# The passes over a long input placed one by one behind the weight splits of a short projection, and a convolution placed behind operand splits

## The chip, the cores and the metric

The kernel runs on one core of a Trainium2 chip. The metric is the device time of one execution in microseconds (us). The engines in the text are PE (TensorE, matmuls), DVE (VectorE), ACT (ScalarE), POOL (GpSimd) and SP (SyncE, which issues the DMA transfers).

## The reference, cut to what matters

One layer of a hybrid encoder is applied to two inputs that share all weights: a long one of 1024 tokens and a short one of 512, each with 16 learned tokens ahead. Everything is float32.

```python
n = rms_norm(h, g_mix)
qa, ka, va, qb, kb, vb = split(n @ w_in)              # one projection, 18 blocks of 128 columns
oa = softmax_attention(rope(rms_norm(qa)), rope(rms_norm(ka)), va)      # grouped queries, 2-D rotary
ob = rms_norm((softmax(qb0 @ kb0) - lam * softmax(qb1 @ kb1)) @ vb)     # differential attention
h = h + concat(oa, ob) @ w_out
n = rms_norm(h, g_ffn)
gate = conv3(n @ w_ff_gate) + conv_b                  # depthwise over positions, width 3
h = h + (gelu(gate) * (n @ w_ff_up)) @ w_ff_down
y = rms_norm(h, g_final)[16:]
```

## The kernel before

**Arithmetic.** A float32 operand is held as a rounded part "hi" and a rest "lo". `split` (L103) makes hi with a copy on ACT (L106) and lo = x - hi with a subtraction on DVE, or on POOL where the caller asks for it (L107). `mm3` (L110) makes a product of three matmuls, hi*hi, hi*lo and lo*hi (L113 to L115). `dense` runs it over the 8 blocks of the contraction, so one product of a weight with a chunk of tokens is 24 matmuls.

**Stages.** First the projection of the short input (s = 1) by itself. Then `merge` alternates the generators of two stages by their estimated work: attention of the short input with the projection of the long one (s = 0, named p0), then attention of the long input with the output product and feed-forward of the short. The long input's output product, its feed-forward (`conv_glu_long`, eleven groups of two feature blocks, with products by the schemes of Winograd and Strassen) and the down product come after.

**Projection.** Eight tiles x of the input are loaded (L217). For each, a *pass* makes xhi on ACT (L223) and xlo on DVE (L224), and squares x on ACT (L227). The short input's squares go into a PSUM bank by matmuls; the long one's are added to a tile acc on POOL (L232), and three matmuls with ones (L241, chunks of 384, 384 and 272 tokens) turn acc into the mean. `rsqrt_newton` (L89) makes the reciprocal root: Ln, Exp and Square on ACT (L95 to L97), two steps on DVE (L98, L99). The 18 weights go one after another, KA, VA, QA, VB and so on in pairs, then KB and QB four times. `load_weight` loads one into w_f (L167), of which there is one buffer here, and splits it into w_hi and w_lo (two buffers each). The queries and keys get their norm and rotary (t at L295, then L258 to L261), the values are transposed on PE by L322 from t (L316).

**Attention.** ps_s = k*q (L406, L407), a running maximum with the copy out of PSUM (p, L408), the exponent (L413), transposes of p (L431), their split (L106, L107) and the product with v (L441 to L446).

**Order.** The program is written stage by stage, and a scheduler with a simulated timeline sets one fixed sequence for each engine; an engine then runs its sequence in order and waits at each instruction for what it needs. `tc.issue_after(ins)` adds an edge to this scheduling: what is written inside it stands behind `ins` where both are on one engine. It adds no wait. PSUM banks in the early stages are mm = 2, s = 3, t = 2, o = 1; the short projection uses s and t, the long one mm alone.

Before, the only such edge for the long passes is this one, the short norm's last steps:

```python
for ins in g.norm_of_short:
    order.enter_context(tc.issue_after(ins))
```

## Time and profile before

| what | value |
|---|---|
| median of 3 runs | 2137.26 us (2137.07 to 2148.71) |
| the profiled execution | 2142.05 us, its span 2140.2 us |
| busy: PE | 2046.2 us, 96% of the span |
| busy: DVE | 1738.0 us, 81% |
| busy: ACT | 1158.9 us, 54% |
| busy: POOL | 556.1 us, 26% |

The busy time of an engine is the sum of what ran on it; what it lacks to the span is waiting. All times of the rows below count from the start of the span. In a row such as "t<-ps_s,rstd", the output stands left of the arrow and the inputs right, by the program's names; L295 is a line of the kernel, often of a helper that many places call. "SPq" is the queue in which SP issues transfers.

### The profile page before, as it was taken

What the parts mean: (1) busy time and instruction counts of PE and PEld (TensorE: products, weight loads), DVE (VectorE), ACT (ScalarE), POOL (GpSimd) and SP (SyncE); (2) the same over time, 40 slices, a digit from 0 to 9 for tenths busy, and PEclk for the clock granted to TensorE, in tenths of its full rate; (3) what the DMA queues carried; (4) which work ended last, traced back from release to release, by engine and by line L of the source; (5) the groups of instructions that cost most, each with busy time, mean ns of one, the idle gap of its engine ahead of it and who ended that gap; (6) DMA issues with size and microseconds to landing.
All of it is one profiled execution on the core that took longest, in us unless ns stands there. A gap on an engine that the chain in (4) does not pass through costs nothing.

```text
span 2140.2 us, 35200 instructions
## 1 busy us (share of the span) xinstructions
PE 2046.2 (96%) x12302; PEld 1830.6 (86%) x12302; DVE 1738.0 (81%) x3786; ACT 1158.9 (54%) x2253; POOL 556.1 (26%) x480
## 2 busy tenths in 40 slices
...
GB/s 248 173 178 169 124 119 161 170 167 237 155 105 48 103 72 71 73 85 112 104 187 87 87 78 151 275 291 226 102 109 89 97 116 84 94 168 253 122 125 126
DMA packets 171426, 296.31 MB, mean 138 GB/s; under 512 B 21456, under 2 KB 90608, under 8 KB 170736
## 3 DMA queue, kind: packets, MB, share of 16 engines
...
## 4 chain that ended last, share of the span: by engine, by line
PE 73%; DVE 14%; DMA 6%; issue 3%; ACT 3%; SPq 1%; POOL 0%; DVEq 0%; ACTq 0%; POOLq 0%
PE ps_mm L115 17%; PE ps_mm L113 17%; PE ps_mm L114 16%; PE ps_t L431 5%; PE ps_s L406 3%; PE ps_s L407 3%; DVE w_lo L107 2%; DVE p L408 2%; PE ps_o L446 1%; PE ps_o L445 1%; PE ps_s L113 1%; PE ps_s L115 1%; PE ps_s L114 1%; DVE acc L941 1%; DVE pt_lo L107 1%
## 5 line engine op out<-in xcount | busy, mean ns | idle before, releaser
L113 PE MATMUL ps_mm<-xhi,w_hi 128*128 128x258 f32 (+3 forms) x1264 | 383.2, 303 | 5.5 <-ACT xhi L106 1.6
L114 PE MATMUL ps_mm<-xlo,w_hi 128*128 128x258 f32 (+3 forms) x1264 | 379.5, 300 | 1.9 <-DVE xlo L224 1.2
L115 PE MATMUL ps_mm<-xhi,w_lo 128*128 128x258 f32 (+3 forms) x1264 | 377.1, 298 | 0.0
L408 DVE TENSOR_SCALAR_CACHE_REDUCE p<-ps_s 114x344 f32<-114x344 f32 (+4 forms) x562 | 257.4, 489 | 32.9 <-PE ps_s L407 16.4
L106 ACT CAST pt_hi<-ps_t 128x512 fp32r<-128x512 f32 (+6 forms) x360 | 170.7, 484 | 164.6 <-PE ps_t L431 138.1
L107 DVE TENSOR_TENSOR w_lo<-w_f,w_hi 128x1024 fp32r<-128x1024 f32 (+1 forms) x182 | 195.8, 1082 | 78.5 <-ACT w_hi L106 76.2
L413 ACT ACTIVATE p<-p,nm 114x1040 f32<-114x1040 f32 (+5 forms) x212 | 215.0, 1015 | 71.1 <-DVE nm L411 70.6
L113 PEld LDWEIGHTS ps_mm<-xhi,w_hi 128*128 128x128 f32 x1264 | 240.2, 190 | 11.7 <-ACT xhi L106 3.9
L114 PEld LDWEIGHTS ps_mm<-xlo,w_hi 128*128 128x128 f32 x1264 | 240.2, 190 | 4.7 <-POOL xlo L107 1.5
L115 PEld LDWEIGHTS ps_mm<-xhi,w_lo 128*128 128x128 f32 x1264 | 239.7, 190 | 0.8 <-DVE w_lo L107 0.2
L106 ACT CAST w_hi<-w_f 128x1024 fp32r<-128x1024 f32 (+1 forms) x199 | 167.6, 856 | 98.1 <-PE ps_mm L114 54.9
L107 DVE TENSOR_TENSOR pt_lo<-ps_t,pt_hi 128x512 fp32r<-128x512 f32 (+4 forms) x312 | 172.2, 561 | 35.7 <-ACT pt_hi L106 34.6
L406 PE MATMUL ps_s<-k,q 128*114 128x348 f32 (+4 forms) x552 | 181.9, 336 | 15.9 <-DVE p L408 13.3
L107 POOL TENSOR_TENSOR a_lo<-gate,a_hi 128x256 fp32r<-128x256 f32 x44 | 43.1, 981 | 558.6 <-ACT a_hi L106 555.6
L431 PE MATMUL ps_t<-ident,p 128*128 128x128 f32 (+7 forms) x1188 | 180.5, 269 | 0.6 <-DVE nm L411 0.2
L113 PE MATMUL ps_s<-xhi,w_hi 128*128 128x256 f32 (+4 forms) x480 | 149.3, 314 | 24.8 <-ACT xhi L223 11.7
L407 PE MATMUL ps_s<-k,q 128*114 128x348 f32 (+4 forms) x552 | 171.7, 317 | 0.0
L431 PEld LDWEIGHTS ps_t<-ident,p 128*128 128x128 f32 (+7 forms) x1188 | 139.7, 135 | 27.7 <-issue 6.8
L115 PE MATMUL ps_s<-xhi,w_lo 128*128 128x256 f32 (+4 forms) x480 | 148.1, 311 | 3.5 <-DMA w_lo<-wo 3.0
L114 PE MATMUL ps_s<-xlo,w_hi 128*128 128x256 f32 (+4 forms) x480 | 148.8, 311 | 0.3
L113 PE MATMUL ps_mm<-t_hi,w_hi 128*128 128x512 f32 (+2 forms) x368 | 142.9, 388 | 0.1
L114 PE MATMUL ps_mm<-t_lo,w_hi 128*128 128x512 f32 (+2 forms) x368 | 142.8, 388 | 0.1
(273 smaller groups left out, 5287.3 us busy)
## 6 DMA issues: line engine op xcount, KB each, us to landing
w_f<-w_gate SPq DMA_DIRECT2D x46, 512.0 KB, 3.3
w_f<-w_up SPq DMA_DIRECT2D x44, 512.0 KB, 3.3
w_f<-w_in SPq DMA_DIRECT2D x36, 512.0 KB, 3.5
...
w_f<-w_down SPq DMA_DIRECT2D x22, 512.0 KB, 3.3
...
```

Of the source, the lines that this page charges most:

```text
L106: nc.scalar.copy(hi, src)
L107: (lo_engine or nc.vector).tensor_tensor(out=lo, in0=src, in1=hi.bitcast(F32), op=ALU.subtract)
L113: nc.tensor.matmul(ps, lhsT=whi, rhs=xhi, start=start, stop=False)
L114: nc.tensor.matmul(ps, lhsT=whi, rhs=xlo, start=False, stop=False)
L115: return nc.tensor.matmul(ps, lhsT=wlo, rhs=xhi, start=False, stop=stop).ins
L406: nc.tensor.matmul(ps, lhsT=q[0], rhs=k[:, c0:c0 + cw], start=True, stop=False)
L407: nc.tensor.matmul(ps, lhsT=q[1], rhs=k[:, c0:c0 + cw], start=False, stop=True)
L408: nc.vector.tensor_scalar(out=p[:, c0:c0 + cw], in0=ps, scalar1=HD ** -0.5, scalar2=-3.0e38, op0=ALU.mult, op1=ALU.max, accum_out=mx[:, i: ...
L413: nc.scalar.activation(p, p, AF.Exp, bias=nm, accum_out=l)
L431: nc.tensor.transpose(tps[:, c:c + M], p[:, k0:k0 + kw], g.ident[:M, :M])
L445: nc.tensor.matmul(o, lhsT=v[:, i, :], rhs=hi, start=i == 0, stop=False)
L446: nc.tensor.matmul(o, lhsT=v[:, i, :], rhs=lo, start=False, stop=False)
```

## The change

Two things are done, both with order edges alone. No instruction is added, taken away or altered.

1. `split` returns its two instructions, and the short projection keeps those of each of its weights. Pass k of the long input is placed behind the split of short weight 2 + (3k)//2, that is behind weights 2, 3, 5, 6, 8, 9, 11 and 12, where all passes were behind the short norm. The split of the long input's first weight goes behind the last of these too, and its first product behind the 25th product of the short projection (`short_products`).
2. In `conv_glu_long`, the up-projection's products are started ahead of the convolution, two of them are fetched, and the convolution's four DVE steps are placed behind the lo parts of the operands that were split by then.

```diff
@@ -1,4 +1,5 @@
 from contextlib import ExitStack, nullcontext
+from itertools import chain
 
 import numpy as np
@@ -72,6 +73,14 @@
     pass
 
 
+def behind(g, *ins):
+
+    es = ExitStack()
+    for i in ins:
+        es.enter_context(g.tc.issue_after(i))
+    return es
+
+
 class Psum:
     def __init__(self, tc, name, **bufs):
         self.es = ExitStack()
@@ -103,8 +112,8 @@
 def split(g, hi, lo, src, lo_engine=None):
 
     nc = g.nc
-    nc.scalar.copy(hi, src)
-    (lo_engine or nc.vector).tensor_tensor(out=lo, in0=src, in1=hi.bitcast(F32), op=ALU.subtract)
+    return (nc.scalar.copy(hi, src).ins,
+            (lo_engine or nc.vector).tensor_tensor(out=lo, in0=src, in1=hi.bitcast(F32), op=ALU.subtract).ins)
 
 
 def mm3(g, ps, whi, wlo, xhi, xlo, start, stop):
@@ -133,7 +142,7 @@
 def split_half(g, wp, src, lo_engine=None):
     hi = wp.tile([P, H], F32R, name="w_hi", tag="w_hi", bufs=HB)
     lo = wp.tile([P, H], F32R, name="w_lo", tag="w_lo", bufs=HB)
-    split(g, hi, lo, src, lo_engine)
+    g.last_split = split(g, hi, lo, src, lo_engine)
     return hi, lo
@@ -167,7 +176,9 @@
     nc.sync.dma_start(out=w, in_=src)
     hi = wp.tile([P, D], F32R, name="w_hi", tag="w_hi", bufs=bufs)
     lo = wp.tile([P, D], F32R, name="w_lo", tag="w_lo", bufs=bufs)
-    split(g, hi, lo, w, lo_engine)
+    passes = split(g, hi, lo, w, lo_engine)
+    if g.splits is not None:
+        g.splits.append(passes)
     return hi, lo
@@ -205,7 +216,12 @@
             out.append(tb)
         return out
 
-    first = load_weight(g, wp, g.w_in[KA], ahead=1)
+    late = [[]] * KT
+    if s == 0:
+
+        late = [g.short_splits[2 + (3 * k) // 2] for k in range(KT)]
+    with behind(g, *late[-1]):
+        first = load_weight(g, wp, g.w_in[KA], ahead=1)
 
     with tc.tile_pool(name=f"ps{s}", bufs=2, side=side, reuse_waits="tile") as sp:
         if s == 1:
@@ -216,10 +232,7 @@
             x = sp.tile([P, n], F32, name="x", tag="x", bufs=2 if s == 0 else 8)
             nc.sync.dma_start(out=x, in_=g.xT[s][k * P:(k + 1) * P, :])
             gk = g.vec[:, V_GMIX + k:V_GMIX + k + 1]
-            with ExitStack() as order:
-
-                for ins in g.norm_of_short:
-                    order.enter_context(tc.issue_after(ins))
+            with behind(g, *late[k]):
                 nc.scalar.activation(xhi[k], x, AF.Copy, scale=gk)
                 nc.vector.scalar_tensor_tensor(out=xlo[k], in0=x, scalar=gk,
                                                in1=xhi[k].bitcast(F32), op0=ALU.mult, op1=ALU.subtract)
@@ -232,16 +245,16 @@
                 nc.gpsimd.tensor_tensor(out=acc, in0=acc, in1=x, op=ALU.add)
         c0, cw = chunks[0]
         first_ps = g.psum.tile(P, cw, tag)
-        dense(g, first_ps, first, xhi, xlo, c0, cw)
+        with behind(g, *g.short_products):
+            last = dense(g, first_ps, first, xhi, xlo, c0, cw)
         for i, (c0, cw) in enumerate(chunks):
             if s == 1:
                 ps = ms[i]
             else:
                 ps = g.psum.tile(P, cw, tag2)
                 nc.tensor.matmul(ps, lhsT=g.ones_d, rhs=acc[:, c0:c0 + cw], start=True, stop=True)
-            last = rsqrt_newton(g, sp, rstd[:, c0:c0 + cw], ps, cw)
-        scaled = nc.vector.tensor_scalar(out=rstd, in0=rstd, scalar1=-0.5, scalar2=None, op0=ALU.mult)
-        g.norm_of_short = [last, scaled.ins]
+            rsqrt_newton(g, sp, rstd[:, c0:c0 + cw], ps, cw)
+        nc.vector.tensor_scalar(out=rstd, in0=rstd, scalar1=-0.5, scalar2=None, op0=ALU.mult)
     es = ExitStack()
     bp = pool(ctx, g, f"pb{s}", 2, side)
     tp = pool(es, g, f"pt{s}", 2, side)
@@ -268,11 +281,13 @@
             nc.sync.dma_start(out=g.qk[s][SLOT[j]][2, :, cc], in_=hi.bitcast(F32))
 
 
-    pending = []
+    pending, products = [], []
 
     def product(w, c0, cw):
         ps = g.psum.tile(P, cw, tag)
         last = dense(g, ps, w, xhi, xlo, c0, cw)
+        if s == 1:
+            products.append(last)
         if pending:
             with tc.issue_after(last):
                 pending.pop()()
@@ -355,6 +370,9 @@
                 ps = product(w, c0, cw)
                 rotary(j, c0, cw, ps, *tab)
                 yield 24 * cw
+    if s == 1:
+
+        g.short_products = [products[24]]
 
 
 def attention(ctx, g, s, side):
@@ -957,24 +975,36 @@
             ps = g.psum.tile(P, 2, "mm")
             nc.tensor.matmul(ps, lhsT=first_sums[i], rhs=g.ones_d[:, 0:2], start=True, stop=True)
             nc.scalar.activation(gate[:, i, 0:1], ps[:, 0:1], AF.Copy, scale=float(D))
+
+
+        raw = [load_whole(up, g, g.w_up[f0 + i], "w_f2") for i in range(2)]
+        products = winograd(g, wp, up, x, raw, 0, H)
+        done, order = [], []
+        for _ in range(2):
+            i, half, ps, rest = next(products)
+            nc.vector.tensor_tensor(out=ps, in0=ps, in1=rest, op=ALU.add)
+            done.append((i, half, ps, None))
+            order += [g.last_split[1:]] * 2
         for i in range(2):
             f = f0 + i
             cw3 = [g.vec[:, V_CW + t * NFF + f:V_CW + t * NFF + f + 1] for t in range(3)]
             cb = g.vec[:, V_CB + f:V_CB + f + 1]
             a = act[:, i]
             nc.scalar.activation(a, gate[:, i, 1:], AF.Identity, scale=cw3[1], bias=cb)
-            nc.vector.scalar_tensor_tensor(out=a, in0=gate[:, i, :N], scalar=cw3[0], in1=a,
-                                           op0=ALU.mult, op1=ALU.add)
-            nc.vector.scalar_tensor_tensor(out=a[:, :N - 1], in0=gate[:, i, 2:], scalar=cw3[2], in1=a[:, :N - 1],
-                                           op0=ALU.mult, op1=ALU.add)
+            with behind(g, *order.pop(0)):
+                nc.vector.scalar_tensor_tensor(out=a, in0=gate[:, i, :N], scalar=cw3[0], in1=a,
+                                               op0=ALU.mult, op1=ALU.add)
+            with behind(g, *order.pop(0)):
+                nc.vector.scalar_tensor_tensor(out=a[:, :N - 1], in0=gate[:, i, 2:], scalar=cw3[2],
+                                               in1=a[:, :N - 1], op0=ALU.mult, op1=ALU.add)
         gelu = nc.scalar.activation(act, act, AF.Gelu)
         if f0 + 2 == NFF:
             with tc.issue_after(gelu.ins):
                 nc.scalar.preload_act_table_set(EXP_LN)
-        raw = [load_whole(up, g, g.w_up[f0 + i], "w_f2") for i in range(2)]
-        for i, half, ps, rest in winograd(g, wp, up, x, raw, 0, H):
+        for i, half, ps, rest in chain(done, products):
             a = act[:, i, half * H:(half + 1) * H]
-            nc.vector.tensor_tensor(out=ps, in0=ps, in1=rest, op=ALU.add)
+            if rest is not None:
+                nc.vector.tensor_tensor(out=ps, in0=ps, in1=rest, op=ALU.add)
             nc.vector.tensor_tensor(out=a, in0=ps, in1=a, op=ALU.mult)
         (x11, x12), (x21, x22) = [[act[:, i, half * H:(half + 1) * H] for half in range(2)] for i in range(2)]
@@ -1289,9 +1319,12 @@
         return st
 
     g.psum = Psum(tc, "psa", mm=2, s=3, t=2, o=1)
-    g.norm_of_short = []
+    g.short_products = []
+
+    g.splits = []
     with ExitStack() as es:
         drain(projection(es, g, 1, "right", "s", "t"))
+    g.short_splits, g.splits = g.splits, None
     with ExitStack() as es0:
         p0 = projection(es0, g, 0, "left", "mm", "mm")
         with ExitStack() as es1:
```

Line numbers shift: L106 and L107 of the kernel before are L115 and L116 in the changed one, L223, L224 and L227 are L236, L237 and L240, L241 is L255, L95 to L99 are L104 to L108, L113 to L115 are L122 to L124, L295 and L316 are L310 and L331, L408 is L426, and L259 and L260 are L272 and L273.

**The start, on DVE,** behind the norm of the short input (rstd_181). The names w_lo_469 and w_lo_555 are of the short weights 2 and 3 (counted from 0), xlo0_1922 and the like are of the long passes. Before:

```order
L243 TENSOR_SCALAR rstd_181<-rstd_181 128x528
L224 SCALAR_TENSOR_TENSOR xlo0_1922<-x_1941,vec_110,xhi0_1914 128x1040
L295 TENSOR_TENSOR t_312<-ps_s_249,rstd_181 128x256
L295 TENSOR_TENSOR t_362<-ps_s_316,rstd_181 128x272
L316 TENSOR_TENSOR t_418<-ps_s_372,rstd_181 128x256
L224 SCALAR_TENSOR_TENSOR xlo1_1923<-x_1946,vec_110,xhi1_1915 128x1040
L107 TENSOR_TENSOR w_lo_469<-w_f_466,w_hi_468 128x1024
L224 SCALAR_TENSOR_TENSOR xlo2_1924<-x_1952,vec_110,xhi2_1916 128x1040
L98 SCALAR_TENSOR_TENSOR hn_343<-ps_t_341,eps_133,hn_343 128x256
L99 SCALAR_TENSOR_TENSOR hn_343<-hn_343,rs_y_344 128x256
L107 TENSOR_TENSOR w_lo_555<-w_f_552,w_hi_554 128x1024
```

Now:

```order
L257 TENSOR_SCALAR rstd_181<-rstd_181 128x528
L310 TENSOR_TENSOR t_312<-ps_s_249,rstd_181 128x256
L310 TENSOR_TENSOR t_362<-ps_s_316,rstd_181 128x272
L331 TENSOR_TENSOR t_418<-ps_s_372,rstd_181 128x256
L116 TENSOR_TENSOR w_lo_469<-w_f_466,w_hi_468 128x1024
L237 SCALAR_TENSOR_TENSOR xlo0_1922<-x_1941,vec_110,xhi0_1914 128x1040
L116 TENSOR_TENSOR w_lo_555<-w_f_552,w_hi_554 128x1024
L237 SCALAR_TENSOR_TENSOR xlo1_1923<-x_1946,vec_110,xhi1_1915 128x1040
L107 SCALAR_TENSOR_TENSOR hn_343<-ps_t_341,eps_133,hn_343 128x256
```

Of the passes one stands behind each w_lo, and the three short t are ahead of them all.

**The end of the short projection, on PE.** The tiles ps_mm_2021 and ps_mm_2029 are the second and third chunk of the long norm, ps_s_1816 is the last short product, ps_mm_2138 the long KA product's second chunk. Before, around the first of the two (the other stands 200 rows later between short products):

```order
L115 MATMUL ps_s_1065<-xhi7_172,w_lo_1033 128x272
L241 MATMUL ps_mm_2021<-acc_1940,ones_d_117 128x384
L113 MATMUL ps_s_1122<-xhi0_165,w_hi_1118 128x256
L114 MATMUL ps_s_1122<-xlo0_173,w_hi_1118 128x256
L115 MATMUL ps_s_1122<-xhi0_165,w_lo_1119 128x256
```

Now:

```order
L123 MATMUL ps_s_1816<-xlo7_180,w_hi_1775 128x272
L124 MATMUL ps_s_1816<-xhi7_172,w_lo_1776 128x272
L255 MATMUL ps_mm_2021<-acc_1940,ones_d_117 128x384
L255 MATMUL ps_mm_2029<-acc_1940,ones_d_117 128x272
L122 MATMUL ps_mm_2138<-xhi0_1914,w_hi_1933 128x384
L123 MATMUL ps_mm_2138<-xlo0_1922,w_hi_1933 128x384
L124 MATMUL ps_mm_2138<-xhi0_1914,w_lo_1934 128x384
```

The two and the long product now follow one another, behind all short products.

**The border of the two attentions, on DVE.** The names w_lo_7000, w_lo_7258 and w_lo_7522 are of the first weights w_out, ps_mm_6815 is the last long product, o_rs_5555 belongs to the end of the short attention, p_6900 to the first softmax of the long one. Before:

```order
L107 TENSOR_TENSOR w_lo_7000<-w_f_6997,w_hi_6999 128x1024
L107 TENSOR_TENSOR w_lo_7258<-w_f_7255,w_hi_7257 128x1024
L98 SCALAR_TENSOR_TENSOR o_rs_5555<-ps_o_5550,o_rs_5555 128x306
L99 SCALAR_TENSOR_TENSOR o_rs_5555<-o_rs_5555,rs_y_5556 128x306
L524 SCALAR_TENSOR_TENSOR o_b_5546<-o_b_5546,gsub_131,o_rs_5555 128x306
L107 TENSOR_TENSOR w_lo_7522<-w_f_7519,w_hi_7521 128x1024
L408 TENSOR_SCALAR p_6900,mx_6901<-ps_s_6902 128x348
L408 TENSOR_SCALAR p_6900,mx_6901<-ps_s_6906 128x348
L408 TENSOR_SCALAR p_6900,mx_6901<-ps_s_6910 128x344
```

Now:

```order
L542 SCALAR_TENSOR_TENSOR o_b_5546<-o_b_5546,gsub_131,o_rs_5555 128x306
L271 TENSOR_TENSOR u_6840<-ps_mm_6815,rope_5921 128x272
L272 TENSOR_TENSOR w_6841<-ps_mm_6815,rope_5923 64x272
L273 TENSOR_TENSOR w_6841<-ps_mm_6815,rope_5923 64x272
L426 TENSOR_SCALAR p_6900,mx_6901<-ps_s_6902 128x348
L426 TENSOR_SCALAR p_6900,mx_6901<-ps_s_6906 128x348
L426 TENSOR_SCALAR p_6900,mx_6901<-ps_s_6910 128x344
L599 MEMSET m_6929 128x1
L426 TENSOR_SCALAR p_7034,mx_7035<-ps_s_7036 128x348
```

The end of the short attention has moved ahead of the last rotary step, and the first of the three w_lo stands fourteen rows behind the first softmax row, where all three were ahead of it.

## Rows read from the trace of the kernel before

**Rows 1.** The page's part 1: busy time, share and instructions of each engine.

```profile
PE 2046.2 (96%) x12302; PEld 1830.6 (86%) x12302; DVE 1738.0 (81%) x3786; ACT 1158.9 (54%) x2253; POOL 556.1 (26%) x480
```

**Rows 2.** Windows: span, then busy us of each engine, PEclk, DMA share, GB/s.

```profile
40.00:60.00 20.00, 16.92 (x113) 16.70 (x114) 17.61 (x24) 11.38 (x19) 10.68 (x8) 0.83 0.58 192
60.00:80.00 20.00, 15.91 (x111) 15.11 (x109) 19.64 (x24) 10.95 (x21) 14.90 (x10) 0.91 0.52 171
100.00:120.00 20.00, 20.00 (x165) 19.90 (x164) 17.42 (x35) 7.93 (x19) 11.99 (x15) 1.00 0.63 203
500.00:530.00 30.00, 11.96 (x43) 10.30 (x44) 12.36 (x34) 9.94 (x18) 2.33 (x6) 0.54 0.97 335
530.00:700.00 170.00, 161.81 (x1097) 141.93 (x1096) 150.24 (x446) 111.92 (x204) 29.77 (x38) 1.00 0.34 105
```

**Rows 3.** Waits of PE, 20 to 130: total us, times, longest.

```profile
PE ps_s L113 <- ACT xhi L223: 4.4, 1, 4.4
PE ps_s L113 <- DVE t L295: 2.3, 1, 2.3
PE ps_s L113 <- ACT w_hi L106: 2.2, 1, 2.2
PE ps_s L113 <- DVE t L316: 1.8, 1, 1.8
PE ps_mm L114 <- DVE xlo L224: 1.2, 1, 1.2
PE ps_s L115 <- DVE w_lo L107: 0.5, 1, 0.5
```

**Rows 4.** Waits of PE, 140 to 400: the largest entry.

```profile
PE ps_mm L322 <- DVE t L316: 4.5, 3, 2.7
```

**Rows 5.** Timeline of PE, SP's queue, ACT and DVE at the border: start, duration, instruction.

```profile
497.85 0.29 PE L115 MATMUL ps_mm<-xhi,w_lo 128*128 128x272 f32 x1
512.49 1.57 SPq L167 DMA_DIRECT2D w_f<-w_out  x2
521.68 1.04 ACT L106 CAST w_hi<-w_f 128x1024 fp32r<-128x1024 f32 x1 [11.24 <-DMA w_f<-w_out]
522.76 1.22 DVE L107 TENSOR_TENSOR w_lo<-w_f,w_hi 128x1024 fp32r<-128x1024 f32 x1 [10.72 <-ACT w_hi L106]
523.90 0.51 DVE L408 TENSOR_SCALAR_CACHE_REDUCE p<-ps_s 128x348 f32<-128x348 f32 x1
```

**Rows 6.** Waits of PE, 495 to 535: the two largest.

```profile
PE ps_s L406 <- DVE p L408: 11.7, 1, 11.7
PE ps_o L518 <- ACT o_sq L516: 2.9, 1, 2.9
```

**Rows 7.** Waits of PE, 1600 to 1900.

```profile
PE ps_mm L115 <- DVE w_lo L107: 3.8, 7, 0.9
```

**Rows 8.** Timeline of SP's queue (first and sixth w_f issue), and the page's landing time.

```profile
40.77 0.33 SPq L167 DMA_DIRECT2D w_f<-w_in  x1
84.25 0.41 SPq L167 DMA_DIRECT2D w_f<-w_in  x1
w_f<-w_in SPq DMA_DIRECT2D x36, 512.0 KB, 3.5
```

**Rows 9.** Groups on DVE and POOL, 20 to 130, and one instruction of DVE's timeline.

```profile
L107 DVE TENSOR_TENSOR w_lo<-w_f,w_hi 128x1024 fp32r<-128x1024 f32 x15 | 23.5, 1564 | 10.1 <-ACT w_hi L106 10.0
L224 DVE SCALAR_TENSOR_TENSOR xlo<-x,vec,xhi 128x1040 fp32r<-128x1040 f32 x8 | 13.8, 1720 | 0.4 <-ACT xhi L223 0.4
L232 POOL TENSOR_TENSOR acc<-acc,x 128x1040 f32<-128x1040 f32 x7 | 18.7, 2674 | 4.0 <-ACT x L227 4.0
37.31 3.43 DVE L107 TENSOR_TENSOR w_lo<-w_f,w_hi 128x1024 fp32r<-128x1024 f32 x1
```

**Rows 10.** Timeline of ACT and DVE: a chunk of the long norm.

```profile
123.26 0.48 ACT L95 ACTIVATE rs_y<-ps_mm,eps 128x272 f32<-128x272 f32 x1
125.59 0.50 DVE L98 SCALAR_TENSOR_TENSOR rstd<-ps_mm,eps,rstd 128x272 f32<-128x272 f32 x1
```

## Prediction

> **What bounds the kernel now.** I read the page's busy times first. TensorE (PE) is busy for 2046.2 us of a 2140.2 us span [rows 1], so only the 94 us in which it stands still, and the stretches in which its clock is down, can be won. Next the windows, to see where that is: PE is short of full in 40:60 and 60:80 (the projection of the short input), again a little up to 400, most of all in 500:530, where it is busy for 11.96 of 30 us, and it is full in 100:120 [rows 2]. Last the chain of waits of PE in each such stretch, to see what it waits for. There are four places.
>
> *The short projection.* Six waits between 20 and 130 us add up to 12.4 us [rows 3]. The longest, 4.4 us, is for a conversion of the **long** input (xhi at L223): an instruction of the long product stands in PE's queue between short products and holds all behind it. The wait of 1.2 us is of the same kind. The others are for DVE (t at L295 and L316) and for the split of the next weight. The clock adds a little: its mean is 0.83 in 40:60 and 0.91 in 60:80 [rows 2], and as there are two levels (2.4 and 1.2 GHz) this is some 6.8 and 3.6 us at the lower. Of these PE was idle for 4.4 and 2.3 us, so half of the rest, 1.2 + 0.7 = 1.9 us, is lost. Together **14.3 us**.
>
> *The middle* (140 to 400 us). The largest entry is 4.5 us for t at L316 [rows 4].
>
> *The border* between attention of the short and attention of the long input. The last long product starts at 497.85 us and ends 0.29 us later; the first softmax step (L408) starts at 523.90 us [rows 5]: 25.8 us. PE's longest wait in it, 11.7 us, is put down to that L408 [rows 6]. L408 had nothing to wait for but its place in the queue: the row ahead of it on DVE is a w_lo that started at 522.76 us after 10.72 us of idling, its w_hi on ScalarE (ACT) had idled 11.24 us for a w_out transfer, and that transfer was issued at 512.49 us [rows 5]. The weight isn't needed there; it stood ahead by order alone.
>
> *The long feed-forward.* Between 1600 and 1900 us PE waits seven times for w_lo, once for each group of features, 3.8 us in all [rows 7].
>
> **The change part by part.** No instruction is added or taken away; instructions are moved, so I cost places.
>
> *1. The long passes, one behind each short split.* Before, xlo0 to xlo2 stand among the first rows behind the short norm on DVE, and w_lo of short weights after them. Now each w_lo stands ahead of its pass, and the long KA product comes in one piece after the last pass. So the 4.4 and the 1.2 us have no cause left. What is late next is the weights' own chain. There is one w_f buffer, so the next load is issued only after the split of the one before: between 40.77 and 84.25 us five weights went by, 8.7 us each, against a landing time of 3.5 us [rows 8]. Without queueing a weight costs 3.5 + 1.04 (w_hi) + 1.22 (w_lo) [rows 5] and about 0.3 to issue: 6.1 us. PE needs for one weight 48 dense and about 5 small matmuls; in 100:120 it did 165 in 20.00 us [rows 2], so 53 x 0.121 = 6.4 us. DVE has its own sum: w_lo takes 1.56 us on average and xlo 1.72 us [rows 9], and it was busy for 19.64 of 20 us in 60:80 [rows 2]. The eight passes (13.8 us of DVE [rows 9]) don't go away, they are spread over eleven weights. I take 6.8 to 7.3 us for a weight, above the 6.4 of PE, because DVE's queue still holds the chain up: about 0.55 x 11 = 6 us of idling. If nothing queues it is 0; at 8.0 us for each weight it is 17.6 us.
>
> The same edge brings a **new wait**. Before, the sums of the long norm (ps_mm_2021, ps_mm_2029) lie some 200 rows apart between short products. Now these two and the next long product stand in a row on PE, with two banks, one of which is still held by the long KA product. Each must wait until Ln, Exp and Square on ACT and one DVE step have read the one before. From the start of Ln at 123.26 us to the end of that DVE step at 125.59 + 0.50 us it took 2.8 us [rows 10] with a short queue on DVE; I take 2.5 us, twice: 5.0 us, and 0.9 us for the clock behind it, about half of what the two stretches above lost. Behind them in PE's queue stand the whole of the long products and the short attention. Were both covered it would be 0. So the loss after is 6 + 5.0 + 0.9 = 12 us against 14.3: **+2 us** gained, from +12 (no queueing, waits half covered) to -9 (8.0 us for each weight).
>
> *2. The middle.* The transposes behind L316 have as many rows of distance as before. Nothing in the order says that 4.5 us goes or grows; **0**, up to 7 either way, for what a different interleaving of the same work may do.
>
> *3. The border.* The diff doesn't name it; it comes of the new order. The tail of the short attention now lies among the last long products, the loads of v and of six q are issued ahead of the w_out loads, and L408 (L426 now) comes directly behind the last rotary step on DVE, with the first w_lo fourteen rows later. Left are about 1.7 us from the last product to the first softmax step (two ps_s matmuls and three short DVE steps). The tail's own matmuls, about 2 us of PE, are still to be done in a place where PE is full: 25.8 - 1.7 - 2 = 22. The three w_lo of 1.22 us that lay in the hole now fall where DVE is busy for 150.24 of 170 us [rows 2]; I charge 2 us. **+20 us**; at most 24 (nothing charged), at least 10 (only the 11.7 us goes, and 1.7 comes).
>
> *4. The convolution behind the next splits* (long feed-forward). From the second group on, the order on every engine is the one of before: there L966 and L968 stood behind that w_lo already. The waits of 3.8 us stay; **0**. Only the first group moves, and no wait of PE lies there.
>
> The Trainium skill bears on part 1. The rows first: w_lo takes 1.22 us at 522.76, with GpSimd (POOL) idle, and 3.43 us at 37.31 beside an addition to acc, of which there are seven of 2.67 us on average [rows 5, 9]. The page "SBUF — State Buffer", section "Who interferes with whom", says that DVE and GpSimd share one pair of ports under an exclusive lock; its section on the two sides adds that the loser is blocked for the whole instruction. By that rule this trace's 2.2 us more is a wait and not a slower step, and it is the third rival.
>
> **The rivals.** (a) *The border doesn't pay.* The q tiles or the short tail could be late themselves: before, PE waited there 2.9 us for o_sq too [rows 6]. Then only part 1 is left, and a few us: about 2133. Against it: v and q are loaded from what was written some rows earlier, and PE has the last products to do meanwhile.
> (b) *Starvation, slower than before.* The long product filled PE's time while short weights were late. Without it PE idles for all that a weight takes beyond 6.4 us. At the 8.7 us of before over the 16 weights left: 16 x 2.3 = 36.8, plus 5.9, minus 14.3 and minus 20: +8.4 us, about 2146. It decides from (14.3 + 20 - 5.9) / 16 = 1.8, that is 8.2 us for each weight. For it: DVE is near full. Against: the rows that made 8.7 us, three xlo in a row and the long split ahead of the short ones, are those that go.
> (c) *Each POOL addition meets the next w_lo.* Now an addition follows every pass, and the next step on the chain is a w_lo. Seven times 2.2 us is 15 us more on the chain: about 2129. For it: 3.43 against 1.22 us; against: after a pass there are some 4.5 us of landing and ACT first, and an addition is over by then.
> (d) *The convolution's part does more than the order shows*, and the waits on w_lo in all groups go: 3.8 us and a little clock, about 2109.
>
> **How the numbers follow.** The profiled execution took 2142.05 us, with 2140.2 us in its span; that is 4.8 us above the median of the three runs, 2137.26. The sum, +2 + 0 + 20 + 0 = 22 to 23 us, taken from the profiled one gives 2119.5; the difference goes by the median: **2114 us**. Chances: forecast 0.57, (a) 0.20, (b) 0.06, (c) 0.09, (d) 0.08. The bounds of the three uncertain parts (+12 to -9, +7 to -7, +24 to +10) put the forecast's own range at 2099 to 2128; (a) and (c) carry it up to 2135, which leaves out (b) and the best ends together. A change of 1%, 21 us, is about what a measurement tells from none, and the forecast lies just beyond it: faster by over 1% (under 2116) is 0.57 x 0.65 and most of (d), some of (a): 0.47; within 1%: 0.48; slower 0.05, as (b) must exceed its own price for that.
>
> **What would show it.** Right: no wait of PE on xhi or xlo of the long input before 125 us; two waits of about 2.5 us on DVE in front of the second and third matmul of the long norm and product; weights' loads 6.8 to 7.3 us apart; no wait over 3 us between 480 and 510 us, and no w_lo of w_out ahead of the first softmax step. Wrong: loads over 8 us apart, or a new long wait at the border, on q or on o_sq, or PE's waits after it grown by what went there.

## The result: slower by a quarter of a per cent, with PE idle as long as before

The changed kernel takes 2145.22 us (median of 20 runs, 2140.34 to 2153.72), the kernel before 2141.16 us beside it (20 runs, 2133.62 to 2151.13). The ratio is 1.0024 with a 95% interval of 1.0013 to 1.0035: slower, by less than the 1% that the chances spoke of, but clear of noise. The forecast of 2114 and its range of 2099 to 2135 missed it.

The profiled execution of the changed kernel is one of its longest, 2153.15 us with a span of 2151.3. Its part 1 of the page, and below it the windows (length, then busy us of PE, PEld, DVE, ACT, POOL, then PEclk, DMA share, GB/s), answer to [rows 1, 2]. The windows are cut at events that both kernels have: the last product of the short projection, the last long product, the first softmax step of the long input, and the first product of the short feed-forward. The changed kernel:

```profile
PE 2056.5 (96%) x12302; PEld 1837.8 (85%) x12302; DVE 1727.4 (80%) x3786; ACT 1158.5 (54%) x2253; POOL 557.0 (26%) x480
0.00:160.60 160.60, 135.74 (x966) 131.04 (x967) 116.92 (x193) 81.08 (x143) 82.72 (x75) 0.95 0.59 197
160.60:514.20 353.60, 336.91 (x2169) 314.45 (x2168) 274.61 (x821) 190.46 (x458) 138.73 (x129) 0.98 0.46 147
514.20:516.80 2.60, 1.27 (x9) 0.99 (x7) 2.51 (x6) 0.51 (x1) 0.98 (x1) 1.00 0.69 216
516.80:711.50 194.70, 178.62 (x1193) 156.07 (x1194) 166.11 (x492) 124.90 (x227) 33.76 (x46) 0.97 0.42 137
```

The same four stretches of the kernel before:

```profile
0.00:157.20 157.20, 137.42 (x987) 132.52 (x988) 121.77 (x199) 83.79 (x150) 81.96 (x75) 0.96 0.60 201
157.20:497.85 340.65, 328.46 (x2125) 308.48 (x2123) 279.76 (x809) 183.76 (x442) 137.46 (x127) 0.98 0.46 149
497.85:523.90 26.05, 8.06 (x33) 6.02 (x31) 8.44 (x15) 7.75 (x14) 3.48 (x8) 0.59 0.91 318
523.90:712.90 189.00, 180.23 (x1212) 159.69 (x1213) 167.09 (x500) 124.85 (x227) 33.24 (x41) 0.98 0.35 111
```

A window's length less PE's busy time is what PE idled. Before it is 19.8, 12.2, 18.0 and 8.8 us; now 24.9, 16.7, 1.3 and 16.1. So the hole at the border is closed, for 16.7 us, and 5.1, 4.5 and 7.3 us of it are given back in the other three: 16.9 us. Over the whole span PE idles 94.8 us, against 94.0.

The 10.3 us by which PE is busy longer don't lie in these stretches. Both traces are cut here at one matmul that has the same number of matmuls ahead of it, 8658 (the first that reads a_hi with 256 columns). The kernel before, then the changed one:

```profile
0.00:1344.32 1344.32, 1282.12 (x8658) 1191.65 (x8659) 1102.35 (x2934) 794.99 (x1543) 297.05 (x295) 0.98 0.41 131
1344.32:2140.20 795.88, 764.11 (x3646) 638.93 (x3644) 635.69 (x853) 363.94 (x710) 259.02 (x185) 0.99 0.46 151
```

```profile
0.00:1345.25 1345.25, 1282.94 (x8659) 1190.07 (x8659) 1088.86 (x2934) 794.34 (x1543) 298.05 (x295) 0.98 0.41 131
1345.25:2151.30 806.05, 773.60 (x3646) 647.77 (x3644) 638.54 (x853) 364.15 (x710) 258.90 (x185) 0.97 0.45 149
```

Up to there the changed kernel is 0.9 us longer and PE idles 62.3 us, against 62.2: gains and losses cancel. The other 10.2 us of this pair lie behind it, in the long feed-forward, where the order differs only in the first group. They are this execution's and not the order's: run 1 below has the order of the changed kernel there, on PE, ACT and POOL to the row, and takes 796.07 us.

The waits of PE in the changed kernel that the forecast speaks of (waited for: us in all, times, longest). The first three are from 20 to 157 us and answer to [rows 3]; all entries there sum up to 17.5 us, where it was 12.4. The next two are from 157 to 500, the next two from 495 to 560 ([rows 6]), the last from 1500 to 1910 ([rows 7]):

```profile
PE ps_s L122 <- DVE t L331: 8.3, 3, 4.4
PE ps_s L122 <- DVE w L273: 6.3, 2, 3.2
PE ps_s L124 <- DVE w_lo L116: 0.5, 1, 0.5
PE ps_mm L255 <- DVE rstd L107: 2.4, 1, 2.4
PE ps_mm L122 <- DVE rstd L107: 2.2, 1, 2.2
PE ps_mm L122 <- ACT xhi L115: 7.2, 7, 2.2
PE ps_s L424 <- DVE p L426: 3.8, 2, 1.9
PE ps_mm L124 <- DVE w_lo L116: 3.6, 6, 0.7
```

The waits for xhi and xlo of the long input are gone, as is the one of 11.7 us. In their place PE waits for short DVE steps (t, w), twice for the long norm (rstd), and behind the border for xhi, the operand of the output product.

**The clock.** Each execution has its granted clock listed. The mean over 20 runs of the changed kernel is 0.9815, that over 113 runs of the kernel before (all calls) 0.9843. Within each of the kernels run here the executions differ in it, and a clock that is lower by 0.001 goes with 1.5 us more time (272 runs, each kernel about its own mean; correlation -0.79). So 0.0028 goes with some 4 us, out of 5.5 us between the two means. Where the changed order would lose it, no profile shows. PE was busy at the lower level for some 56 us in the profile before and 71 us in the changed kernel's; but up to the cut above it is 39.6 us before and 35.0 now (42.5 and 35.1 in runs 1 and 4, which have the changed order up to there), and behind the cut 16.6 and 36.2.

### The profile page after: what moved, and what is told of

Its sections match the earlier page's. It is cut to its first block, busy times and chain, and to the rows that moved or that the text cites. A ratio compares the mean times of both kernels' runs of the same rounds, so it can differ in the third digit from the quotient of the medians.

```text
span 2151.3 us, 35214 instructions
## 1 busy us (share of the span) xinstructions
PE 2056.5 (96%) x12302; PEld 1837.8 (85%) x12302; DVE 1727.4 (80%) x3786; ACT 1158.5 (54%) x2253; POOL 557.0 (26%) x480
## 4 chain that ended last, share of the span: by engine, by line
PE 74%; DVE 13%; DMA 5%; issue 3%; ACT 3%; POOL 1%; SPq 1%; DVEq 0%; ACTq 0%; POOLq 0%
PE ps_mm L122 17%; PE ps_mm L124 17%; PE ps_mm L123 17%; PE ps_t L449 5%; PE ps_s L424 3%; PE ps_s L425 3%; PE ps_s L122 2%; PE ps_s L124 2%; PE ps_s L123 2%; DVE w_lo L116 2%; PE ps_o L464 2%; DVE p L426 2%; PE ps_o L463 1%; DMA w_lo<-wo 1%; DVE acc L959 1%
## 5 line engine op out<-in xcount | busy, mean ns | idle before, releaser
L122 PE MATMUL ps_mm<-xhi,w_hi 128*128 128x258 f32 (+3 forms) x1264 | 384.1, 304 | 12.7 <-ACT xhi L115 7.6
L124 PE MATMUL ps_mm<-xhi,w_lo 128*128 128x258 f32 (+3 forms) x1264 | 376.9, 298 | 0.0
L426 DVE TENSOR_SCALAR_CACHE_REDUCE p<-ps_s 114x344 f32<-114x344 f32 (+4 forms) x562 | 257.3, 489 | 30.5 <-PE ps_s L425 20.0
L115 ACT CAST pt_hi<-ps_t 128x512 fp32r<-128x512 f32 (+6 forms) x360 | 170.1, 483 | 161.8 <-PE ps_t L449 135.6
L122 PEld LDWEIGHTS ps_mm<-xhi,w_hi 128*128 128x128 f32 x1264 | 239.9, 190 | 19.0 <-ACT xhi L115 10.7
L116 DVE TENSOR_TENSOR w_lo<-w_f,w_hi 128x1024 fp32r<-128x1024 f32 (+1 forms) x182 | 191.9, 1061 | 72.0 <-ACT w_hi L115 71.4
L124 PEld LDWEIGHTS ps_mm<-xhi,w_lo 128*128 128x128 f32 x1264 | 239.5, 190 | 0.9 <-DVE w_lo L116 0.2
L115 ACT CAST w_hi<-w_f 128x1024 fp32r<-128x1024 f32 (+1 forms) x199 | 167.7, 856 | 109.5 <-PE ps_mm L123 63.1
L116 DVE TENSOR_TENSOR pt_lo<-ps_t,pt_hi 128x512 fp32r<-128x512 f32 (+4 forms) x312 | 172.3, 562 | 37.8 <-ACT pt_hi L115 36.4
L116 POOL TENSOR_TENSOR a_lo<-gate,a_hi 128x256 fp32r<-128x256 f32 x44 | 42.0, 956 | 552.0 <-ACT a_hi L115 532.4
L122 PE MATMUL ps_s<-xhi,w_hi 128*128 128x256 f32 (+4 forms) x480 | 151.2, 318 | 28.3 <-DVE t L331 8.3
L124 PE MATMUL ps_s<-xhi,w_lo 128*128 128x256 f32 (+4 forms) x480 | 150.1, 314 | 4.3 <-DMA w_lo<-wo 3.6
L122 PE MATMUL ps_mm<-t_hi,w_hi 128*128 128x512 f32 (+2 forms) x368 | 144.6, 394 | 1.7 <-ACT t_hi L115 1.7
```

The lines of the kernel that those rows point to most:

```text
L115: return (nc.scalar.copy(hi, src).ins, (lo_engine or nc.vector).tensor_tensor(out=lo, in0=src, in1=hi.bitcast(F32), op=ALU.subtract).ins)
L116: (lo_engine or nc.vector).tensor_tensor(out=lo, in0=src, in1=hi.bitcast(F32), op=ALU.subtract).ins)
L122: nc.tensor.matmul(ps, lhsT=whi, rhs=xhi, start=start, stop=False)
L124: return nc.tensor.matmul(ps, lhsT=wlo, rhs=xhi, start=False, stop=stop).ins
L426: nc.vector.tensor_scalar(out=p[:, c0:c0 + cw], in0=ps, scalar1=HD ** -0.5, scalar2=-3.0e38, op0=ALU.mult, op1=ALU.max, accum_out=mx[:, i: ...
```

## The experiments

Theory A: the gain at the border is real, and given back by waits that the new order makes: POOL's additions that hold up short DVE steps, the norm's two bank waits, and a slow start behind the border. The rivals are given run by run. The table has PE's idle us by stage (worked out as above from each profile; where the first long softmax step comes ahead of the last long product, the border is empty and only the stretch behind it counts, so that the column ahead of it holds some of the long attention too) and the median, the ratio to the kernel before with its interval, and the mean granted clock of the runs.

| kernel | short proj. | to last long product | border and 190 us behind | rest | all | median us | ratio | clock |
|---|---|---|---|---|---|---|---|---|
| before | 19.8 | 12.2 | 26.8 | 35.3 | 94.0 | 2141.16 | 1 | 0.984 |
| changed | 24.9 | 16.7 | 17.4 | 35.8 | 94.8 | 2145.22 | 1.0024 (1.0013 to 1.0035) | 0.982 |
| 1 projection's part alone | 23.9 | 16.3 | 14.7 | 41.1 | 96.0 | 2144.33 | 1.0020 (1.0005 to 1.0036) | 0.982 |
| 2 norm in other banks | 23.1 | 17.3 | 17.8 | 39.5 | 97.7 | 2152.50 | 1.0052 (1.0033 to 1.0070) | 0.981 |
| 3 border alone | 21.1 | 12.9 | 23.9 | 37.4 | 95.2 | 2146.69 | 1.0028 (1.0009 to 1.0048) | 0.982 |
| 4 first group's order | 22.6 | 16.8 | 16.8 | 34.9 | 91.0 | 2144.79 | 1.0025 (1.0010 to 1.0040) | 0.982 |
| 5 changed, no additions | 15.6 | 22.0 | 10.9 | 36.4 | 84.8 | 2135.84 | 0.9974 (0.9957 to 0.9991) | 0.984 |
| 6 before, no additions | 14.9 | 15.5 | 19.3 | 38.9 | 88.5 | 2137.01 | 0.9979 (0.9962 to 0.9997) | 0.984 |
| 7 passes late | 23.0 | 12.2 | 14.1 | 37.1 | 86.3 | 2138.02 | 0.9973 (0.9956 to 0.9989) | 0.986 |
| 8 one pass for each weight | 22.8 | 23.0 | 14.9 | 35.8 | 96.5 | 2152.45 | 1.0055 (1.0038 to 1.0072) | 0.981 |
| 9 additions in pieces | 21.1 | 16.2 | 16.0 | 37.0 | 90.2 | 2142.44 | 1.0013 (0.9994 to 1.0031) | 0.983 |
| 10 late, in pieces | 23.7 | 21.5 | 11.9 | 37.1 | 94.3 | 2151.77 | 1.0049 (1.0031 to 1.0066) | 0.982 |
| 11 changed, additions on DVE | 18.6 | 22.7 | 9.9 | 37.2 | 88.4 | 2136.99 | 0.9986 (0.9969 to 1.0004) | 0.984 |
| 12 before, additions on DVE | 14.8 | 12.1 | 26.5 | 37.7 | 91.0 | 2137.76 | 0.9983 (0.9968 to 0.9998) | 0.983 |
| 13 late, additions on DVE | 23.7 | 22.7 | 12.6 | 35.2 | 94.1 | 2153.81 | 1.0056 (1.0036 to 1.0076) | 0.981 |

In what each kernel's PE does the runs agree: span less idling less half the busy time at the lower clock is 2018 to 2024 us in all of them.

**1. The projection's part alone.** The changed kernel with the convolution block of before:

```diff
-            with behind(g, *order.pop(0)):
-                nc.vector.scalar_tensor_tensor(out=a, in0=gate[:, i, :N], scalar=cw3[0], in1=a,
-                                               op0=ALU.mult, op1=ALU.add)
+            nc.vector.scalar_tensor_tensor(out=a, in0=gate[:, i, :N], scalar=cw3[0], in1=a,
+                                           op0=ALU.mult, op1=ALU.add)
...
```

> The changed kernel with the convolution of the kernel before, so only the passes and the long weight are moved. Theory A (all of the change's effect comes from the projection's part, since the convolution's part leaves the order as it was but for one DVE row of the first group): the time of the changed kernel, 5 us above the kernel before, ratio 1.001 to 1.004. Theory B (the convolution's part costs what was lost in the first group of the long feed-forward, 5.6 us in the traces): no slower than the kernel before, ratio 0.998 to 1.001.

1.0020 against 1.0024: the projection's part has all of the effect. The other half alone, on the kernel before, was not run.

**2. The norm's sums in other banks.**

```diff
-                ps = g.psum.tile(P, cw, tag2)
+                ps = g.psum.tile(P, cw, "t")
                 nc.tensor.matmul(ps, lhsT=g.ones_d, rhs=acc[:, c0:c0 + cw], start=True, stop=True)
```

> The changed kernel, with the long norm's three sums in the two banks of the transposes in place of the long product's own two. Theory A (the two waits of 2.4 and 2.2 us for the norm's steps are lost time, with some clock behind them): they go, and the kernel is 4.6 to 6.5 us faster than the changed one, about 2139 to 2141, even with the kernel before. Rival (DVE is the limit in this stretch, and PE loses the same time a little later): 2144 to 2146, with other waits on DVE grown by what went.

The two waits are gone, and the kernel is slower still. Its waits of PE, first from 157 to 500, then from 500 to 530 us:

```profile
PE ps_s L424 <- DMA q<-qk: 4.5, 1, 4.5
PE ps_s L424 <- DVE p L426: 7.9, 1, 7.9
```

A wait of 4.5 us for a q tile stands where the two were, and the scheduler, whose simulated times have moved, has put the first w_lo of w_out ahead of the first softmax step again: 7.9 us. Theory A's sum did not come, nor the rival's (DVE as the limit): what came instead is a transfer and an order. So the run doesn't tell what the two waits cost by themselves.

**3. The border alone.** The kernel before, with the first three w_out splits behind the first softmax of the long input:

```diff
+            with ExitStack() as order:
+                for ins in (g.first_softmax if j < 3 else []):
+                    order.enter_context(tc.issue_after(ins))
                 w = load_weight(g, wp, g.w_out[j], bufs=wb)
```

> The kernel before, with the first three w_out splits put behind the first softmax of the long attention on ACT and DVE; nothing else moved. Theory A (the hole at the border is lost time): the wait of 11.7 us shrinks to under 4 us and the kernel is 7 to 12 us faster than before, 2129 to 2134. Rival (the work that stood in the hole, splits and tiles of the output product, has to be done next anyhow with DVE near full, so PE waits for it after the border): the wait goes but the time stays within 3 us of before.

Its windows from the last long product to the first softmax step and from there to the first product of the short feed-forward:

```profile
499.80:513.70 13.90, 7.31 (x32) 5.80 (x31) 4.86 (x11) 4.72 (x11) 3.04 (x6) 0.71 0.88 284
513.70:712.50 198.80, 181.49 (x1193) 159.55 (x1193) 167.36 (x497) 124.48 (x227) 29.47 (x43) 0.96 0.40 127
```

The hole is 13.90 us long in place of 26.05, and PE idles 6.6 us in it, 11.4 less. Then it idles 17.3 us in place of 8.8. The largest wait of PE there, and the DVE row that held it up:

```profile
PE ps_s L406 <- DVE m L583: 6.0, 1, 6.0
521.69 0.43 DVE L107 TENSOR_TENSOR xlo<-m,xhi 128x258 fp32r<-128x258 f32 x1 [5.85 <-ACT xhi L106]
```

The profile puts the wait down to the row m at 522.50, which stands among the softmax steps (L408) from 522.03 on; all of these stand behind xlo in DVE's queue. xlo belongs to the output product and isn't needed by the softmax; it is ahead by order alone, as w_lo was before. So the edge put one such row behind, and the next took its place. Of the 11.4 us only 2.9 are kept at the border and the sum of the kernel is 95.2. The rival was right that tiles of the output product are waited for next; what a border without any such row is worth, the run doesn't show. The time is not less but more (1.0028), outside the 3 us of the rival too; the profiled execution (2142.11 us, one of the shorter ones) doesn't show why.

**4. The first group of the long feed-forward.** There the changed kernel had a wait of 1.73 us for t_hi, and 17 us at the lower clock behind it. The run puts the additions into gate behind the operands' splits:

```diff
-                nc.vector.tensor_tensor(out=gate[:, i, t0:t0 + cw], in0=ps, in1=rest, op=ALU.add)
-                for _ in range(3):
+                for _ in range(7):
                     next(late, None)
+                with behind(g, *(g.late_last if f0 + c0 == 0 else [])):
+                    nc.vector.tensor_tensor(out=gate[:, i, t0:t0 + cw], in0=ps, in1=rest, op=ALU.add)
```

> The changed kernel, with the DVE row order of the first group of the long feed-forward put back near that of before: the last parts of the long input's operands (t_lo) ahead of the additions into gate. Theory A (the order there made the wait of 1.73 us for t_hi, and the clock fell for 17 us behind it): the wait is under 0.5 us, the granted clock of the stretch is back near that of before, and the time is 4 to 7 us under the changed kernel's, 2138 to 2141. Rival (the low clock there was an accident of that one execution): 2144 to 2146, the stretch in the trace as short as before or as long, whatever the order.

The stretch from the second norm to the first gate column, in one window each of the changed kernel, of run 1 and of this run, in three fences:

```profile
1458.40:1492.60 34.20, 30.75 (x171) 29.17 (x169) 26.67 (x40) 18.01 (x41) 4.17 (x3) 0.80 0.66 232
```

```profile
1455.90:1485.70 29.80, 25.16 (x170) 24.07 (x169) 26.01 (x40) 17.09 (x41) 3.53 (x3) 0.95 0.77 270
```

```profile
1454.50:1482.10 27.60, 24.36 (x160) 23.40 (x159) 24.03 (x35) 16.46 (x40) 2.91 (x2) 0.94 0.86 297
```

Run 1, whose order there is the changed kernel's, has 29.8 us and a clock of 0.95, where the changed kernel's profile has 34.2 us and 0.80. Run 6, which has the order of the kernel before on PE and ACT there, takes 804.5 us behind the cut at 8658 matmuls, 8.7 more than that kernel's profile, with PE busy at the lower level for 30.3 us. So the low clock was that execution's, not the order's. With the order put back the median is 2144.79: the rival holds.

**5 and 6. Without POOL's additions,** in the changed kernel and in the kernel before:

```diff
             elif k:
-                nc.gpsimd.tensor_tensor(out=acc, in0=acc, in1=x, op=ALU.add)
+                pass
```

> The changed kernel without the seven POOL additions of the long norm (its sum of squares holds the first of eight tiles only). Theory A (in the short projection a POOL addition of 2.4 us holds up a DVE step with two operands in SBUF, three times one that PE waits for: L272 of 2.48 and 2.54 us where 0.42 is usual, L319 of 2.74): PE's waits between 20 and 157 us fall from 17.5 us to 8 to 11, and the stage ends 5 to 9 us earlier. Rival (DVE is late because w_lo and xlo stand ahead of the short steps in its order, or because a weight lands late, whatever POOL does): waits within 2 us of those of the changed kernel.

> The kernel before without the seven POOL additions of the long norm (its sum of squares holds the first of eight tiles only), to tell what the additions cost there. Theory A (before, the additions fell mostly beside xlo and w_lo of the long input and cost PE less): waits of PE between 20 and 157 us fall by under 4 us from 12.4. Rival (the additions cost the same in both kernels): they fall by as much as in the changed kernel, 6 to 9 us.

First how an addition is seen in the changed kernel: the timeline of POOL, DVE and PE (start, duration, instruction, idle time before it and what ended that).

```profile
38.37 2.43 POOL L245 TENSOR_TENSOR acc<-acc,x 128x1040 f32<-128x1040 f32 x1 [10.36 <-ACT x L240]
38.08 0.48 DVE L319 SCALAR_TENSOR_TENSOR t<-t,gain,hn 128x256 f32<-128x256 f32 x1
38.59 2.48 DVE L272 TENSOR_TENSOR w<-t,rope 64x256 f32<-64x256 f32 x1
41.09 0.85 DVE L273 TENSOR_TENSOR w<-t,rope 64x256 f32<-64x256 f32 x1
41.98 0.44 DVE L331 TENSOR_TENSOR t<-ps_s,rstd 128x272 f32<-128x272 f32 x1
42.57 0.55 PE L122 MATMUL ps_s<-xhi,w_hi 128*128 128x256 f32 x1 [4.43 <-DVE t L331]
```

L272 works on 64 x 256 elements and started 0.22 us behind the addition. It took 2.48 us and ended 0.27 us after the addition's end at 40.80. The t for which PE waited 4.43 us stands two rows behind it in DVE's queue. The same instructions as groups, 20 to 150 us (busy, mean ns), changed kernel, kernel before and run 5 in three fences:

```profile
L272 DVE TENSOR_TENSOR w<-t,rope 64x256 f32<-64x256 f32 x5 | 6.3, 1258 | 0.2
L319 DVE SCALAR_TENSOR_TENSOR t<-t,gain,hn 128x272 f32<-128x272 f32 x5 | 4.9, 979 | 0.1
```

```profile
L259 DVE TENSOR_TENSOR w<-t,rope 64x256 f32<-64x256 f32 x5 | 2.1, 421 | 0.2
L304 DVE SCALAR_TENSOR_TENSOR t<-t,gain,hn 128x272 f32<-128x272 f32 x5 | 2.8, 570 | 0.1
```

```profile
L272 DVE TENSOR_TENSOR w<-t,rope 64x256 f32<-64x256 f32 x5 | 2.1, 421 | 0.2
L319 DVE SCALAR_TENSOR_TENSOR t<-t,gain,hn 128x272 f32<-128x272 f32 x5 | 2.6, 527 | 0.1
```

1258 ns with the additions, 421 without, and 421 in the kernel before, where they meet other steps. Of the seven additions in the changed kernel five hold a short step of the keys' and queries' norm or rotary for some 2 us. The page "SBUF — State Buffer" of the Trainium skill, section "Who interferes with whom", says that DVE and GpSimd share a port pair under an exclusive lock; the timeline agrees, with 2.48 us against 0.42.

The kernel before has the same holds. One of its seven additions, with the two DVE steps that start within it:

```profile
66.42 2.64 POOL L232 TENSOR_TENSOR acc<-acc,x 128x1040 f32<-128x1040 f32 x1 [0.72 <-ACT x L227]
66.70 0.49 DVE L98 SCALAR_TENSOR_TENSOR hn<-ps_t,eps,hn 128x272 f32<-128x272 f32 x1
67.22 2.14 DVE L99 SCALAR_TENSOR_TENSOR hn<-hn,rs_y 128x272 f32<-128x272 f32 x1
```

L99 (0.43 to 0.45 us elsewhere) reads two tensors in SBUF and is held; L98 reads one of its two from PSUM and takes its usual time. That is so throughout: six steps with a tensor in PSUM start within an addition there and take 0.27 to 0.49 us, as elsewhere. Four of the seven additions hold a short norm or rotary step, three a w_lo or xlo. Added up over the steps that start within an addition, beyond their time elsewhere, DVE is held for 11.2 us before and 10.6 us now. So the hold isn't new, nor larger; what differs is what waits behind it.

Without the additions the changed kernel goes from 1.0024 to 0.9974; up to the end of the short projection (145 us in place of 160) PE's waits from 20 us on are 8.6 us in place of 17.5, as theory A had it, and it idles 9.3 us less in that stage. The kernel before goes from 1 to 0.9979 and idles 4.9 us less there, between the theory's 4 and the rival's 6. Left without additions, the two kernels are even in that stage (15.6 and 14.9 us of idling) and in time (2135.84 and 2137.01). By the ratios the additions cost the changed kernel 0.0050, some 11 us, and the kernel before 0.0021, some 4 us. That difference would cover the loss of 5 us, but it is hardly larger than its noise (each ratio is good to some 3 or 4 us), and the profiles, one execution each, don't bear it out: up to the cut at 8658 matmuls the additions' absence saves 8.7 us in the changed kernel and 9.9 in the kernel before. So it is shown that the additions cost both kernels time, and the changed one more of it in the short projection; that they are what makes it slower is not. The order of some DVE rows changes too when they go.

**7 and 8. The passes elsewhere.** Behind weights 10 to 17 (run 7), and behind 2 to 9 (run 8, with 2 + k):

```diff
-        late = [g.short_splits[2 + (3 * k) // 2] for k in range(KT)]
+        late = [g.short_splits[10 + k] for k in range(KT)]
```

> The changed kernel with the eight passes behind the splits of short weights 10 to 17 in place of 2 to 12, so behind the keys and queries of the second group, that have fewer DVE steps for each weight. Theory A (passes and additions among the first ten weights are what PE waits for): waits between 20 and 110 us fall to under 7 us and the stage ends 4 to 8 us earlier; the long product's passes may then be waited for, a few us. Rival (PE loses to the weights' own chain, one w_f buffer, whatever the passes do): waits within 2 us of those of the changed kernel.

> The changed kernel with the eight passes behind the splits of short weights 2 to 9, one for each, in place of every 1.5 weights. Theory A (each pass with its addition costs PE about 2 us where it meets the steps of the first ten weights): 1 to 4 us more waiting of PE before 160 us than in the changed kernel. Rival (only the sum of the work counts, not its places): the same within 1 us.

Run 7 is the one order of the passes that beats both kernels clear of noise: 2138.02, 0.9973 (0.9956 to 0.9989). Its waits of PE from 20 to 157 us, and its windows up to the last short product, the last long product and the first product of the short feed-forward:

```profile
PE ps_s L122 <- DVE w L273: 9.4, 4, 3.7
PE ps_s L122 <- DVE t L331: 1.0, 1, 1.0
```

```profile
0.00:155.20 155.20, 132.24 (x943) 127.31 (x944) 109.45 (x190) 79.69 (x139) 77.38 (x72) 0.96 0.60 198
155.20:511.80 356.60, 344.43 (x2204) 321.16 (x2203) 278.68 (x839) 194.84 (x465) 144.50 (x135) 0.99 0.48 153
511.80:705.40 193.60, 179.53 (x1183) 155.83 (x1182) 163.37 (x478) 122.08 (x224) 33.83 (x44) 0.97 0.41 133
```

From 20 to 110 us the waits fall from 11.2 to 7.1 us and the stage ends 5.5 us earlier, near theory A's 7 and within its 4 to 8 (with 23 matmuls fewer in it). But the short projection as a whole idles 23.0 us, hardly less than the changed kernel's 24.9: what went returns later as waits for w (L273), 9.4 us in all. What is gained lies after it: 12.2 us of idling up to the last long product in place of 16.7, with no wait for the long norm, and 14.1 behind in place of 17.4. Run 8 doesn't lose in the short projection (22.8) but between it and the last long product, where PE waits for the softmax steps of the short attention, as in runs 5, 10, 11 and 13 (157 to 500 us):

```profile
PE ps_s L424 <- DVE p L426: 9.4, 6, 3.0
```

In the changed kernel that entry is 1.7 us. So run 7's gain and run 8's loss lie mostly in a stage that neither expectation named.

**9, 10 and 11. Smaller additions, and additions on DVE.**

```diff
-                nc.gpsimd.tensor_tensor(out=acc, in0=acc, in1=x, op=ALU.add)
+                for a0 in range(0, n, 260):
+                    nc.gpsimd.tensor_tensor(out=acc[:, a0:a0 + 260], in0=acc[:, a0:a0 + 260], in1=x[:, a0:a0 + 260], op=ALU.add)
```

In run 11 the one instruction stays and is issued by nc.vector in place of nc.gpsimd.

> The changed kernel with each POOL addition of the long norm in four pieces of 260 columns in place of one of 1040. Theory A (a DVE step that meets an addition is held until the whole POOL instruction ends): a step is held for at most one piece, 0.6 to 0.8 us in place of 2; DVE's L272 at 2.5 us no longer occurs, PE's waits between 20 and 157 us fall by 2 to 6 us, and the kernel is 2 to 6 us faster than the changed one, 2140 to 2143. Rival (the two engines share their throughput, and only the sum of columns counts): the waits stay within 1.5 us of the changed kernel's, and the time is 2144 to 2147 or, with the fixed cost of more instructions, slower.

> The passes behind weights 10 to 17, as in the run with late passes, and each POOL addition in four pieces. Theory A: 1 to 4 us faster than that run's 2138, 2133 to 2137, since the additions that still meet the rotary steps of keys and queries hold them for a quarter of the time. Rival: 2137 to 2140.

> The changed kernel with the seven additions on DVE in place of POOL, so that nothing of them runs beside a DVE step, but DVE has seven instructions of some 1.3 us more. Theory A (a POOL addition costs DVE about 2.1 us where it meets a step, DVE itself needs 1.3 us for it): between 0 and 5 us faster than the changed kernel, 2140 to 2145. Rival (DVE is the limit of this stage by its sum, and 9 us more on it are 9 us later): 2150 to 2155.

The additions as a group on POOL, changed kernel and run 9, then on DVE in run 11 with the rotary step beside them:

```profile
L245 POOL TENSOR_TENSOR acc<-acc,x 128x1040 f32<-128x1040 f32 x7 | 17.1, 2436 | 19.2 <-ACT x L240 19.2
```

```profile
L246 POOL TENSOR_TENSOR acc<-acc,x 128x260 f32<-128x260 f32 x28 | 25.3, 933 | 20.6 <-ACT x L240 20.6
```

```profile
L245 DVE TENSOR_TENSOR acc<-acc,x 128x1040 f32<-128x1040 f32 x7 | 8.7, 1240 | 1.2 <-ACT x L240 1.2
L272 DVE TENSOR_TENSOR w<-t,rope 64x256 f32<-64x256 f32 x5 | 3.4, 679 | 0.2
```

In pieces the additions take 25.3 us of POOL in place of 17.1. No rotary step between 20 and 160 us is longer than 0.93 us any more, where two took 2.48 and 2.54, so a step is held until the POOL instruction ends that it met, as theory A says. The kernel is some 3 us faster than the changed one and idles 3.8 us less in the short projection: theory A's direction at the lower end, with an interval (0.9994 to 1.0031) that overlaps the changed kernel's. On DVE an addition takes 1.24 us, the rotary step 679 ns, and the kernel is 8 us faster than the changed one, more than the 5 that was expected. Run 10 missed both of its expectations. It idles 21.5 us in the middle, as run 8 does; but so do runs 5 and 11, which are quicker than the changed kernel, so that alone isn't the reason, and the run tells nothing of pieces.

**12 and 13. The same on the kernel before, and both remedies.**

> The kernel before with the seven additions on DVE in place of POOL. Theory A (before, the additions met mostly xlo and w_lo of the long input, and cost little): 9 us more work on a DVE that is at 17 to 19 of 20 us there gives back what the additions cost, 2138 to 2144, ratio 0.999 to 1.002. Rival (the additions cost PE the same in both kernels): as much faster than its parent as the changed kernel was, 8 us, 2131 to 2134.

> The changed kernel with the passes behind weights 10 to 17 and the additions on DVE. Theory A (both remedies take away the same thing, additions of POOL that meet short steps of the first ten weights): they don't add up, 2135 to 2140. Rival (they take away different losses): 2128 to 2133.

Run 12 (nc.vector in the kernel before): 0.9983, a gain of 0.0017, just beyond theory A's range and short of the rival's, where the same edit gives the changed kernel 0.0038 (1.0024 to 0.9986). Theory A's ground doesn't hold: three of the seven additions met xlo or w_lo there, four a short step. With the additions on DVE the two kernels are again even, 2136.99 and 2137.76. In the short projection they aren't even (18.6 and 14.8 us of idling). Run 13 is slower than either and missed both expectations, with 22.7 us idle in the middle, as in run 8. The two remedies don't add up; why is not shown.

## Why the prediction was wrong, point by point

**What bounds the kernel** was read rightly, but for two things. The wait at the border was costed as if the hole were a loss by itself; run 3 closed 11.4 us of it and kept 2.9. And the clock's price in the short projection, 1.9 us, took 4.4 and 2.3 us of its low stretches as idle; PE was busy for 5.5 and 3.4 us in them, and half of that is some 4.4 us.

**Step 1, the passes,** failed in size and sign, and with it the forecast: +2 us was forecast, and PE idles 5.1 us more in the short projection and 4.5 more behind it. Its mechanisms stood as forecast for the long input (the waits for xhi and xlo went, and two waits of 2.43 and 2.16 us for the norm came, against 2.5 each). The failed term is the 6 us of idling in the first weights, with the weights' own chain as its cause: the trace has 17.5 us there, and of these only 0.5 are for a weight's split; the rest are short DVE steps of the norm, the rotary and the values (t, w, hn). The term took PE's need as 6.4 us and 6.8 to 7.3 us for a weight; the loads are issued as far apart as before. Two of them with eight between, and the window from one to the other:

```profile
36.00 0.33 SPq L176 DMA_DIRECT2D w_f<-w_in  x1
114.17 0.33 SPq L176 DMA_DIRECT2D w_f<-w_in  x1
36.00:114.17 78.17, 65.11 (x476) 62.87 (x476) 69.89 (x102) 44.87 (x85) 46.58 (x37) 0.93 0.51 171
```

78.2 us for nine weights, 8.7 us each, where before it was 8.7 too [rows 8]: 7.2 us of it PE is busy, at a mean clock of 0.93, and 1.45 us it idles. The DVE sum in it counted w_lo and xlo, but not that an addition behind each pass can hold a norm or rotary step. Run 5 shows the share of that: without additions 8.6 of the 17.5 us are left. Rival (c) had the mechanism and its price of about 2 us, at the wrong place: it let the additions meet w_lo, and argued that they would be over by then.

**Step 2, the middle:** 0, with a bound of 7; the idling there rose by 4.5 us. The norm's two waits that step 1 had costed are 4.6 us by themselves; the other entries came out about even.

**Step 3, the border:** 22 us of gain in the hole were reckoned, of which 18.0 - 1.3 = 16.7 were idling, and 2 charged for three w_lo. PE was also busy in the hole for 8.06 us, at a mean clock of 0.59, where 2 us were counted. Measured behind it are 7.3 us more; the largest wait there is 7.2 us for xhi, the operand of the output product, where the kernel before waited 0.8 us. ACT in turn waited for the tiles m of it (510 to 560 us):

```profile
ACT xhi L115 <- DMA m<-oT: 3.2, 6, 1.2
```

The net of the step is 16.7 - 7.3 = 9.4, just under its lower bound of 10: the failed term is the 2 us charged for what the hole had covered.

**Step 4, the convolution:** right. The waits on w_lo are 3.6 us (3.8 before), and run 1 shows no effect.

**The clock** was costed, among the losses, at 0.9 us behind the norm's waits and at nothing elsewhere. By the executions' listed clocks some 4 us of the measured difference go with it. But no run changed the clock alone, and the profiles don't place it: up to the cut at 8658 matmuls, where the change lies, PE is busy at the lower level for less time than before in two of the three profiles with the changed order. So the trace shows why 22 us of gain didn't come, idling that moved; what makes the median 4 us longer stays open.

**Rival (a)** was half right: the border paid 9.4 of 20 us, and what was late there was xhi, not q or the short tail. **Rival (b)** has the right side of zero and even the right time, 2146, by the weights' period of 8.7 us. That is luck: PE waits for splits of weights for 0.5 us in the stage and not 36.8, and the border gained 9.4 and not 20 us.

What stays open is why some orders (runs 5, 8, 10, 11, 13) idle 21 to 23 us before the last long product and others 12 to 17. They have PE wait for the softmax steps of the short attention in common, 9 to 12 us; no run moved that by itself. Of these, runs 8, 10 and 13 are slower than the changed kernel, runs 5 and 11 quicker.
